# A four-layer mixed decoder trunk on one core: six edits to the order of layer 0's small VectorE work

## The chip, the cores and the metric

The kernel runs on 1 core of one Trainium2 chip. The metric is the device time of an execution in microseconds, lower is better. The engines are named TensorE (PE in rows), VectorE (DVE), ScalarE (ACT), GpSimd (POOL) and SyncE (SP), which only issues transfers here.

## The reference

A trunk of four layers over a sequence of 256 tokens of width 1024, float32. Each layer normalizes, mixes tokens, multiplies by a SiLU gate, projects out, and adds the normalized result to the stream. Layer 0 is native sparse attention, layers B, C and D are differential, dilated and stick-breaking attention. Layer 0, which the change is about:

```python
q, kc, vc, ks, vs, kw, vw, gl, z = split_cols(u @ w_in, A_SPLITS)   # 16 heads, 4 KV heads
kcmp = compress(kc, pos_k, w1_k, w2_k); vcmp = compress(vc, pos_v, w1_v, w2_v)   # 15 blocks
p_c = masked_softmax(einsum(qb, kcmp) - slopes * dist, dist >= 0); o_c = einsum(p_c, vcmp)
p_s = masked_softmax(einsum(qb, ksel) - slopes * dist, dist >= 0); o_s = einsum(p_s, vsel)
p_w = masked_softmax(einsum(qb, kwin) - slopes * dist, mask);      o_w = einsum(p_w, vwin)
o = sum(sigmoid(gl) * stack([o_c, o_s, o_w]))                       # over the three branches
return (o * silu(z)) @ w_out
```

At 256 tokens all four selection blocks of 64 are among the 16 that may be selected, and the window of 512 covers the sequence, so the selected and the window branch are both plain causal attention.

## The kernel before

**Weights.** They stream from memory by transfers that SyncE issues into the buffers `raw` (five of them; a buffer is free again when its piece's low part has been computed). Each piece of 128 x 1024 is split in two for float32 accuracy: ScalarE writes the rounded high part `whi` (L133), VectorE the low part `wlo` = raw - whi (L72). The activations are split likewise (`uth`, `utl`), and a projection is a triple of matmuls per step, L226, L227 and L228, where only L228 reads `wlo`. A projection of 256 columns (`push_proj`) has 16 steps over two pieces, and at a piece's step 0 the low parts that are due are issued.

**Layer 0.** Its attention runs in eight units p = 0 to 7 (`nsa_unit`), two heads each, with one KV group g = p // 2 for two units. `cmp_front(g)` makes the scores against the compressed keys (L789, reduced by VectorE at L793), whose softmax is a list of small operations `CHALF`: a first half L799 to L804, ended by ScalarE's exponential L805, and a second half L807 to L811. A unit's front has three slots: `first` (scores L846 and L847 of query block 0, both heads), `second` (block 1, head 0) and `finish` (block 1, head 1). Each score bank is followed by VectorE's masked maximum (L325, tile mxa) and ScalarE's exponential with its sum (L327, tile la). `scale` makes ten operations: the reciprocal and the gate product of the sums (L865) and eight scalings of P (L871). They are put in the list `SCALE` and run inside the next unit's `first`. Its back transposes P (L332), lets ScalarE evict the transposes (L172, tile PT), and weights the values (L348, L351, L888). Two score banks and two transpose banks rotate.

**Between them.** The steps of q and z projections lie in the queue `fq` and fill TensorE: `fill()` pops some after each slot, and `need(g)` pops until the projection that a unit needs lies at least six steps back. q's high part is ScalarE's L685, its low part VectorE's L686, `later` by five steps. The silu of z ends in L434; `Gate.go` multiplies the result by it (L385), and `Gate.split` cuts the product into the high and low part of the output projection's operand (L394). The output projection begins at L291.

**What sets the order.** TensorE keeps the source's order everywhere. In layer 0 (`st["own"]`), VectorE keeps it too, so the place where the source issues a small operation is its place in VectorE's queue; `later(n, f)` issues f after n more popped steps. ScalarE's, GpSimd's and SyncE's order is set by a scheduler from priorities, and outside layer 0 VectorE's as well. `low_parts(n)` issues n of the low parts that are due. In layer B, POOL's L565 finishes a mask for layer C from VectorE's L563 and L564, and L1012 and L181 make the norm for L1017 and L1024.

Of the kernel before, what the change touches and what calls it, by code (L numbers as in the profile page):

```python
# [37 lines left out]
def trunk(ctx, tc, I, out):  # L38
    nc = tc.nc
    PE, ACT, DVE, POOL = nc.tensor, nc.scalar, nc.vector, nc.gpsimd  # L40
# [37 lines left out]
    def low_parts(n):  # L78

        for i in sorted(low)[:n]:  # L80
            low.pop(i)()

    def later(n, f):

        if st["own"]:
            waiting.append((plan["count"] + n, f))
        else:
            f()
# [51 lines left out]
    def take(n):  # L140
        st["next"] += n
        return list(range(st["next"] - n, st["next"]))

    def free(*idx):
        for i in idx:
            parts.pop(i)
            st["parts" if seq[i][1] else "held"] -= 1
# [77 lines left out]
    def mm3(o, sh, sl, mh, ml, first, last):  # L225
        PE.matmul(o, sh, mh, start=first, stop=False)  # L226
        PE.matmul(o, sh, ml, start=False, stop=False)  # L227
        PE.matmul(o, sl, mh, start=False, stop=last)  # L228

    fq = deque()  # L230
    plan = {"slots": 1, "keep": 0, "count": 0}
    ready = {}
# [8 lines left out]
    def pop():  # L241
        fq.popleft()()
        plan["count"] += 1
        overdue()
# [5 lines left out]

    def need(i):

        while fq and (i not in ready or plan["count"] < ready[i] + 6):
            pop()

    def push_proj(use, q=fq, idx=None):

        t = {}
        idx = idx or take(2)

        def step(c, k):
            if c == 0 and k == 0:
                t["o"] = ps.tile([128, 2, 256], F32, name="mm", bufs=NMM)
            for i, at in ((idx[c], 0), (idx[c] + 1, 0)):
                if k == at and i in low:
                    low.pop(i)()
            wh, wl = parts[idx[c]]
            mm3(t["o"][:, c, :], wh[:, k, :], wl[:, k, :], uT[0][:, k, :], uT[1][:, k, :], k == 0, k == 7)
            if k == 7:
                free(idx[c])  # L270
                if c == 1:
                    use(t["o"])
                advance()

        for c in range(2):
            for k in range(8):
                q.append(lambda c=c, k=k: step(c, k))
# [76 lines left out]
    class Gate:  # L354
# [18 lines left out]

        def have_o(self, p):
            self.o.add(p)
            self.go()

        def go(self):
            while self.ready < 4:
# [188 lines left out]
    idx = take(8)  # L568
# [108 lines left out]
    def keep_q(o, g):  # L677


        for j in range(2):  # L680
            r, other = HALF[j], HALF[1 - j]
            hs = slice(4 * g + j, 4 * g + j + 3, 2)
            hi, sc = t["q"][r, hs, :], cq[r, 2 * g:2 * g + 1]
            with tc.high_priority(offset=EARLY):
                ACT.activation(hi, o[r], AF.Copy, scale=sc)  # L685
            later(5, lambda r=r, other=other, hs=hs, hi=hi, sc=sc: DVE.scalar_tensor_tensor(  # L686
                t["q"][other, hs, :], o[r], sc, hi.bitcast(F32), op0=OP.mult, op1=OP.subtract))
        ready[g] = plan["count"]

# [78 lines left out]
    for g in range(1, 4):  # L768
        push_proj(lambda o, g=g: keep_q(o, g))
        ga.push(g - 1)  # L770
# [9 lines left out]
    CS, PTC, CHALF, SCALE = {}, {}, [], []  # L780
# [32 lines left out]
    def mixed(*lists):  # L813

        lists = [deque(x) for x in lists]
        while any(lists):
            for x in lists:
                if x:
                    x.popleft()()
# [8 lines left out]
    def nsa_unit(p):  # L828
        g, i = divmod(p, 2)
        t = {}  # L830

        def start():
            need(g)
            t["P"] = {(j, br): work.tile([128, 384], F32, name="P", bufs=8) for j in range(2) for br in range(2)}
            t["l"], t["mx"] = small(8, "la", 3), small(8, "mxa", 3)

        def scores_of(b, js):
            if b == 0:
                start()
            n = 128 * (b + 1)  # L840
            S = {}
            for j in js:
                s = ps.tile([128, 512], F32, name="S", bufs=NSB)
                s = s[:, 0:2 * n].rearrange("p (a n) -> p a n", a=2)
                q = qT[:, 2 * p + j, b * 128:(b + 1) * 128]
                PE.matmul(s, q, KH[:, g, :, 0:n], start=True, stop=False)  # L846
                PE.matmul(s, q, KL[g // 2][:, g % 2, :, 0:n], start=False, stop=True)  # L847
                S[j] = s
            for j in js:
                for br in range(2):  # L850
                    x = (j * 2 + br) * 2 + b
                    softmax(S[j][:, br, :], causal[i], SLA[4 * g + j], 128 * b, 128 * b + n, t["P"][j, br],
                            t["mx"][:, x:x + 1], t["l"][:, x:x + 1])
# [37 lines left out]

        def first():
            scores_of(0, (0, 1))
            mixed(*(x.pop(0) for x in (SCALE, CHALF) if x))

        def second():
            scores_of(1, (0,))
            if CHALF:
                mixed(CHALF.pop(0))
            low_parts(1)  # L900

        front = [first, second, finish]
        back = [lambda: trans(0), lambda: trans(1), pvs]
# [349 lines left out]
```

## Time and profile before

| | |
|---|---|
| median of 3 runs | 579.51 us (578.88 to 580.09) |
| the profiled execution | 579.91 us, span 578.2 us, mean TensorE clock 0.995 of full speed |
| TensorE busy | 559.3 us (97%) |
| VectorE busy | 418.6 us (72%) |
| ScalarE busy | 335.0 us (58%) |
| GpSimd busy | 41.9 us (7%) |
| chain that ended last | TensorE 80%, VectorE 9%, issue 5%, ScalarE 2% |
| low parts L72 | 153, mean 1.206 us |

A busy share is an average over four layers; the stretches of layer 0's attention, from about 66 to 162 us, have to be read alone. The granted clock has two levels, 1.2 and 2.4 GHz, and the profile gives a stretch's mean as a share of the higher.

### The profile page before, as it was taken

Reading aid. Unit: us, or ns where it says so; the run is one execution under the profiler, and the core shown is the slowest. Engines: PE = TensorE matmul, PEld = TensorE weight load, DVE = VectorE, ACT = ScalarE, POOL = GpSimd, SP = SyncE. Lnnn points to the kernel's source line nnn. Section 1 sums busy time; section 2 is a strip of 40 time slices with the busy share of each in tenths; the row PEclk is TensorE's granted clock in tenths of the full one; section 3 lists DMA queues with packets and bytes.
Section 4 is the critical chain, followed back from the end, with each engine's and each line's share of the span. In section 5 each row is a group of like instructions: output and inputs, shape, how many; then the busy total and the mean of one; then the engine's idle time right before and its main releaser. Section 6 shows DMA issues by size and latency. Waiting matters only on the chain.

```text
span 578.2 us, 10454 instructions
## 1 busy us (share of the span) xinstructions
PE 559.3 (97%) x3930; PEld 495.3 (86%) x3930; DVE 418.6 (72%) x927; ACT 335.0 (58%) x719; POOL 41.9 (7%) x89
## 2 busy tenths in 40 slices
PE   7999989999999999999999999999999999999995
PEld 6997878777788799999988789999987898899984
DVE  5883696898857886777965887758548878788632
ACT  6742678788825466567643474757524855666410
POOL 1900000000101100000410100000001000000000
PEclk9999989999999999999999999999999999999999
DMA  9774632322444596443451577443525784332012
GB/s 294 259 246 152 249 110 75 129 91 86 144 154 147 177 332 210 147 147 110 146 158 62 183 270 275 150 143 117 176 73 183 257 289 140 120 108 73 2 37 73
DMA packets 27779, 90.96 MB, mean 157 GB/s; under 512 B 4560, under 2 KB 5200, under 8 KB 27728
## 3 DMA queue, kind: packets, MB, share of 16 engines
q1 hardware_dynamic: 26144, 86.09, 44.2%
q10 hardware_dynamic: 1584, 4.20, 2.3%
q8 instruction: 31, 0.51, 0.4%
q14 instruction: 20, 0.16, 0.1%
HBM read 89.22 MB, written 1.05 MB: 156 GB/s over the span
## 4 chain that ended last, share of the span: by engine, by line
PE 80%; DVE 9%; issue 5%; ACT 2%; POOL 1%; DMA 1%; SPq 0%; POOLq 0%; DVEq 0%; ACTq 0%
PE mm L226 15%; PE mm L227 14%; PE mm L228 14%; PE mm L293 7%; PE mm L292 7%; PE mm L291 7%; DVE wlo L72 4%; PE S L342 3%; PE pt L332 3%; PE o L348 2%; PE o L697 1%; DVE P L325 1%; PE pt L214 1%; DMA h<-in_x_dram 1%; ACT whi L133 1%
## 5 line engine op out<-in xcount | busy, mean ns | idle before, releaser
L226 PE MATMUL mm<-uth,whi 128*128 128x256 f32 x736 | 217.9, 296 | 0.0
L72 DVE TENSOR_TENSOR wlo<-raw,whi 128x1024 fp32r<-128x1024 f32 (+1 forms) x153 | 182.0, 1206 | 41.6 <-ACT whi L133 41.1
L227 PE MATMUL mm<-utl,whi 128*128 128x256 f32 x736 | 208.1, 283 | 0.0
L228 PE MATMUL mm<-uth,wlo 128*128 128x256 f32 x736 | 208.1, 283 | 0.0
L133 ACT ACTIVATE whi<-raw 128x1024 fp32r<-128x1024 f32 (+1 forms) x153 | 156.9, 1044 | 65.9 <-PE mm L227 33.2
L226 PEld LDWEIGHTS mm<-uth,whi 128*128 128x128 f32 x736 | 140.8, 191 | 14.2 <-issue 13.3
L227 PEld LDWEIGHTS mm<-utl,whi 128*128 128x128 f32 x736 | 141.0, 192 | 0.9
L228 PEld LDWEIGHTS mm<-uth,wlo 128*128 128x128 f32 x736 | 140.7, 191 | 0.0
L291 PE MATMUL mm<-whi,qT 128*128 128x512 f32 x128 | 50.4, 394 | 0.0
L292 PE MATMUL mm<-whi,kT 128*128 128x512 f32 x128 | 49.9, 390 | 0.0
L293 PE MATMUL mm<-wlo,qT 128*128 128x512 f32 x128 | 49.9, 390 | 0.0
L291 PE MATMUL mm<-whi,uth 128*128 128x512 f32 (+1 forms) x112 | 42.5, 380 | 0.0
L293 PE MATMUL mm<-wlo,uth 128*128 128x512 f32 (+1 forms) x112 | 42.1, 376 | 0.0
L292 PE MATMUL mm<-whi,utl 128*128 128x512 f32 (+1 forms) x112 | 42.0, 375 | 0.0
L327 ACT ACTIVATE P<-P,mxa 128x128 f32<-128x128 f32 (+1 forms) x64 | 28.4, 446 | 10.6 <-DVE mxa L325 10.5
L325 DVE CUSTOM_DVE_ANT_0 P<-S,mask 128x128 f32<-128x128 f32 (+1 forms) x96 | 29.1, 352 | 7.4 <-PE S L847 5.1
L456 ACT ACTIVATE junk<-mm 128x512 bf16<-128x512 f32 x16 | 9.5, 595 | 42.7 <-PE mm L293 42.7
L332 PE MATMUL pt<-ident,P 128*128 128x128 f32 x180 | 28.3, 280 | 1.7 <-ACT PT L172 0.8
L172 ACT ACTIVATE PT<-pt 128x384 f32<-128x384 f32 x58 | 26.1, 482 | 4.1 <-PE pt L332 3.7
L293 PEld LDWEIGHTS mm<-wlo,qT 128*128 128x128 f32 x128 | 24.0, 188 | 5.0
L291 PEld LDWEIGHTS mm<-whi,qT 128*128 128x128 f32 x128 | 24.1, 188 | 4.7
L292 PEld LDWEIGHTS mm<-whi,kT 128*128 128x128 f32 x128 | 24.1, 188 | 4.7
(206 smaller groups left out, 748.5 us busy)
## 6 DMA issues: line engine op xcount, KB each, us to landing
raw<-in_a_t_dram SPq DMA_DIRECT2D x24, 512.0 KB, 4.4
raw<-in_b_t_dram SPq DMA_DIRECT2D x24, 512.0 KB, 5.0
raw<-in_d_t_dram SPq DMA_DIRECT2D x24, 512.0 KB, 4.6
raw<-in_c_t_dram SPq DMA_DIRECT2D x20, 512.0 KB, 5.6
raw<-in_w_dram SPq DMA_DIRECT2D x8, 512.0 KB, 4.8
raw<-in_a_o_dram SPq DMA_DIRECT2D x8, 512.0 KB, 3.4
raw<-in_b_v_dram SPq DMA_DIRECT2D x8, 512.0 KB, 5.9
raw<-in_b_o_dram SPq DMA_DIRECT2D x8, 512.0 KB, 3.5
```

Of the source, the lines that this page charges most:

```text
L72: lo_of = (POOL if on_pool else DVE).tensor_tensor(lo, t, hi.bitcast(F32), op=OP.subtract)
L133: ACT.activation(hi, t, AF.Copy)
L172: ACT.activation(dst, src, AF.Copy)
L226: PE.matmul(o, sh, mh, start=first, stop=False)
L227: PE.matmul(o, sh, ml, start=False, stop=False)
L228: PE.matmul(o, sl, mh, start=False, stop=last)
L291: PE.matmul(o, sh, wh[:, j, c0:c1], start=k == 0, stop=False)
L292: PE.matmul(o, sl, wh[:, j, c0:c1], start=False, stop=False)
L293: PE.matmul(o, sh, wl[:, j, c0:c1], start=False, stop=k == 7)
L325: DVE.tensor_tensor_reduce(out=P[:, c0:c1], in0=S, in1=mask[:, c0:c1], scale=-slope, scalar=BIG, op0=OP.add, op1=OP.min, accum_out=mx)
L327: ACT.activation(P[:, c0:c1], P[:, c0:c1], AF.Exp, bias=mx, scale=-1.0, accum_out=l)
L332: PE.transpose(pt[:, i, :], P[:, i * 128:(i + 1) * 128], ident)
```

## The change

Six numbers or places in the source:

1. `need` asks for nine steps between a projection and its use, not six. It stands in every layer.
2. In `push_proj` the low part of the next piece is issued at step 3 of the current one, not at step 0.
3. `Gate.have_o` issues the gate product three steps later, not at once.
4. q's low part comes eight steps later, not five.
5. `first` runs the first six operations of `SCALE` (two for the sums, four scalings of branch 0) alone, and mixes only the other four with `CHALF`'s first half. Before, all ten were mixed.
6. `second` issues no low part where there is a `CHALF` half to run, and two where there is none. Before, it issued one in either case.

```diff
     def need(i):
 
-        while fq and (i not in ready or plan["count"] < ready[i] + 6):
+        while fq and (i not in ready or plan["count"] < ready[i] + 9):
             pop()
...
-            for i, at in ((idx[c], 0), (idx[c] + 1, 0)):
+            for i, at in ((idx[c], 0), (idx[c] + 1, 3)):
                 if k == at and i in low:
                     low.pop(i)()
...
         def have_o(self, p):
             self.o.add(p)
-            self.go()
+            later(3, self.go)
...
-            later(5, lambda r=r, other=other, hs=hs, hi=hi, sc=sc: DVE.scalar_tensor_tensor(
+            later(8, lambda r=r, other=other, hs=hs, hi=hi, sc=sc: DVE.scalar_tensor_tensor(
...
             scores_of(0, (0, 1))
-            mixed(*(x.pop(0) for x in (SCALE, CHALF) if x))
+            ops = SCALE.pop() if SCALE else []
+            mixed(ops[:6])
+            mixed(ops[6:], CHALF.pop(0) if CHALF else [])
...
             if CHALF:
                 mixed(CHALF.pop(0))
-            low_parts(1)
+            else:
+                low_parts(2)
```

On VectorE, at the start of the units: L724 and L727 prepare the compressed branch's second layer, L739 and L747 end it, L793 is the first reduction of unit 0's compressed scores, L325 its first masked maximum. This is one piece of the difference.

```order
 L686 SCALAR_TENSOR_TENSOR qT<-mm,cq,qT 64x2x256 x2
-L72 TENSOR_TENSOR wlo<-raw,whi 128x1024
 L724 COPY P<-pt 128x120
 L727 COPY zw<-pt 128x240 x2
+L72 TENSOR_TENSOR wlo<-raw,whi 128x1024
 L739 SCALAR_TENSOR_TENSOR kc<-S,kc 128x4x15
 L747 TENSOR_TENSOR v<-o,bm 60x256 x4
 L793 TENSOR_REDUCE cs<-S 128x120
-L72 TENSOR_TENSOR wlo<-raw,whi 128x1024
 L325 ISA P,mxa<-S,mask 128x128
```

One low part moved behind the copies, and the one ahead of the first maximum left.

On ScalarE, in the same place (L685 is q's high part, L327 the exponentials of unit 0, L805 that of its compressed scores):

```order
 L685 ACTIVATE qT<-mm,cq 64x2x256 x2
-L133 ACTIVATE whi<-raw 128x1024
-L327 ACTIVATE P,la<-P,mxa 128x128 x4
+L327 ACTIVATE P,la<-P,mxa 128x128 x4
+L133 ACTIVATE whi<-raw 128x1024
 L805 ACTIVATE cs<-cs 128x120
-L327 ACTIVATE P,la<-P,mxa 128x256 x2
-L133 ACTIVATE whi<-raw 128x1024
-L327 ACTIVATE P,la<-P,mxa 128x256 x2
+L327 ACTIVATE P,la<-P,mxa 128x256 x4
```

The high part L133 moved from ahead of the four exponentials to between them and L805. In unit 2 it is alike: the rows from L685 to L327 there, before and after.

```order
L685 ACTIVATE qT<-mm,cq 64x2x256 x2
L172 ACTIVATE PT<-pt 128x384 x2
L805 ACTIVATE cs<-cs 128x120
L133 ACTIVATE whi<-raw 128x1024
L172 ACTIVATE PT<-pt 128x384 x2
```

```order
L685 ACTIVATE qT<-mm,cq 64x2x256 x2
L172 ACTIVATE PT<-pt 128x384 x2
L133 ACTIVATE whi<-raw 128x1024
L172 ACTIVATE PT<-pt 128x384 x2
L805 ACTIVATE cs<-cs 128x120
```

L805 moved behind the high part and the second pair of evictions.

On VectorE, at the end of the units, where L940 to L944 (three more in the changed source) make layer B's lambda from a small load: the rows of before, then of after.

```order
L72 TENSOR_TENSOR wlo<-raw,whi 128x1024
L940 ISA P,lam<-P 128x64
L940 ISA lam 128x1
L865 RECIPROCAL la<-la 128x8
L865 TENSOR_TENSOR la<-la,gate 128x8
L871 TENSOR_SCALAR P<-P,la 128x128
...
L434 SCALAR_TENSOR_TENSOR zw<-zw,mm 128x512
L943 TENSOR_TENSOR lam<-lam 128x1
L385 SCALAR_TENSOR_TENSOR oT<-oT,zw 128x512
L394 TENSOR_TENSOR kT<-oT,qT 128x512 x3
```

```order
L72 TENSOR_TENSOR wlo<-raw,whi 128x1024
L434 SCALAR_TENSOR_TENSOR zw<-zw,mm 128x512
L943 ISA P,lam<-P 128x64
L943 ISA lam 128x1
L385 SCALAR_TENSOR_TENSOR oT<-oT,zw 128x512
L865 RECIPROCAL la<-la 128x8
...
L865 TENSOR_TENSOR la<-la,gate 128x8
L871 TENSOR_SCALAR P<-P,la 128x128
...
L394 TENSOR_TENSOR kT<-oT,qT 128x512 x3
```

The last silu and a gate product moved from behind unit 7's scaling to ahead of it.

## Rows read from the trace of the kernel before

**Rows 1.** Busy times by stretch: start:end us, length, each engine's busy us, TensorE's clock, DMA.

```profile
70.00:80.00 10.00, 7.62 (x57) 7.02 (x56) 9.65 (x36) 6.37 (x18) 0.00 (x0) 1.00 0.28 96
...
120.00:130.00 10.00, 8.96 (x71) 7.32 (x71) 9.79 (x39) 7.98 (x25) 0.00 (x0) 1.00 0.36 107
```

**Rows 2.** TensorE's waits, whole run: tile and line, releaser: us in total, times, longest.

```profile
PE S L846 <- DVE mxa L325: 4.3, 5, 2.1
...
PE pt L1024 <- DVE ob L1017: 1.1, 1, 1.1
```

**Rows 3.** TensorE's timeline, units 0 to 5: start, us, line op, idle before, releaser.

```profile
67.86 0.66 PE L735 MATMUL S<-P,w 128*128 128x60 f32 x4 [0.53 <-DVE P L724]
...
76.57 0.28 PE L226 MATMUL mm<-uth,whi 128*128 128x256 f32 x1
...
76.93 0.28 PE L226 MATMUL mm<-uth,whi 128*128 128x256 f32 x1
...
80.18 0.36 PE L846 MATMUL S<-kT,qT 128*128 128x256 f32 x1 [2.13 <-DVE mxa L325]
...
105.66 0.47 PE L846 MATMUL S<-kT,qT 128*128 128x512 f32 x1 [0.80 <-DVE mxa L325]
...
125.76 0.47 PE L846 MATMUL S<-kT,qT 128*128 128x512 f32 x1 [0.62 <-DVE mxa L325]
...
128.83 0.92 PE L332 MATMUL pt<-ident,P 128*128 128x128 f32 x6 [0.42 <-ACT PT L172]
```

**Rows 4.** Busy times by stretch, around the lower clock.

```profile
81.40:84.80 3.40, 3.10 (x14) 2.84 (x14) 3.33 (x19) 2.21 (x8) 0.00 (x0) 0.53 0.48 159
```

**Rows 5.** VectorE's timeline, units 0 and 1.

```profile
71.31 1.21 DVE L72 TENSOR_TENSOR wlo<-raw,whi 128x1024 fp32r<-128x1024 f32 x1
72.44 0.28 DVE L325 CUSTOM_DVE_ANT_0 P<-S,mask 128x128 f32<-128x128 f32 x1
...
77.71 1.51 DVE L686 SCALAR_TENSOR_TENSOR qT<-mm,cq,qT 64x512 fp32r<-64x512 f32 x2
```

**Rows 6.** ScalarE's timeline, units 0 to 3.

```profile
72.44 1.06 ACT L133 ACTIVATE whi<-raw 128x1024 fp32r<-128x1024 f32 x1
...
74.94 0.29 ACT L805 ACTIVATE cs<-cs 128x120 f32<-128x120 f32 x1
...
97.39 0.88 ACT L172 ACTIVATE PT<-pt 128x384 f32<-128x384 f32 x2
98.29 0.30 ACT L805 ACTIVATE cs<-cs 128x120 f32<-128x120 f32 x1
98.50 1.04 ACT L133 ACTIVATE whi<-raw 128x1024 fp32r<-128x1024 f32 x1
```

**Rows 7.** VectorE's timeline, before unit 3's maxima.

```profile
103.27 1.22 DVE L72 TENSOR_TENSOR wlo<-raw,whi 128x1024 fp32r<-128x1024 f32 x1
104.41 0.68 DVE L385 SCALAR_TENSOR_TENSOR oT<-oT,zw 128x512 f32<-128x512 f32 x1
```

**Rows 8.** Timeline, last q low parts and the scores that read them.

```profile
132.56 1.53 DVE L686 SCALAR_TENSOR_TENSOR qT<-mm,cq,qT 64x512 fp32r<-64x512 f32 x2
...
134.06 1.04 PE L789 MATMUL S<-kc,qT 128*128 128x32 f32 x8
```

**Rows 9.** Timeline, VectorE at layer 0's tail, then TensorE's first output projection.

```profile
150.65 0.23 DVE L940 CUSTOM_DVE_ANT_0 P<-P 128x64 f32<-128x64 f32 x1 [1.21 <-DMA P<-in_b_lambda_dram]
...
153.30 1.93 DVE L871 TENSOR_SCALAR P<-P,la 128x128 f32<-128x128 f32 x8
...
161.56 0.40 PE L291 MATMUL mm<-whi,qT 128*128 128x512 f32 x1
```

**Rows 10.** Timeline, VectorE's mask row and GpSimd's behind it, layer B.

```profile
287.54 0.35 DVE L564 TENSOR_SCALAR P<-P 128x384 f32<-128x384 int32 x1
...
288.03 2.47 POOL L565 TENSOR_TENSOR mask<-mask,P 128x384 f32<-128x384 f32 x1 [4.15 <-DVE P L564]
```

## The prediction

> **What bounds the kernel now.** I read the busy times by stretch first. TensorE is busy almost all of the span, so a change of order can save only its idle time and the time at the lower clock. From 70 to 80 us it is busy for 7.62 of 10 us while VectorE is busy for 9.65, and from 120 to 130 for 8.96 against 9.79 [rows 1]: here, in layer 0, VectorE sets the pace. The list of TensorE's waits says the same. Its score matmuls (L846) wait 4.3 us in five places for VectorE's mxa, which is the row maximum whose reading frees the score bank, and in layer B L1024 waits 1.1 us once [rows 2]. These, with what each stall drags behind it, are about all that can be had. The timeline gives each stall its place: 0.53 at L735, then at L846 2.13 (unit 1), 0.80 (unit 3) and 0.62 (unit 5), with 0.75 left for the two others of the five, and 0.42 at a transposition L332 that waits for ScalarE [rows 2, 3]. In all 5.2 us. From 81.4 to 84.8 the granted clock is 0.53, so mostly at 1.2 GHz, after the stretch with the two longest stalls; 3.10 us of matmuls there would take about half at 2.4 GHz [rows 4].
>
> **Units 0 and 1: -0.93.** The low part L72 that stood before L735's source now comes behind it, so 0.53 goes. The next L72 leaves the front of the first softmax: its 1.13 (71.31 to 72.44, where the maxima begin) comes off VectorE's chain [rows 3, 5]. That is 1.66. Some is given back on ScalarE, which the change moves too. Before, L133 (72.44) stood ahead of the four exponentials; now it stands between them and the exponential L805 of the compressed branch, which VectorE needs for L807 [rows 6]. ScalarE cannot begin the four before L685 ends, so L805 falls only some 0.9 earlier and VectorE idles about 0.73: 1.66 - 0.73 = 0.93. One L72 and the q low parts of 77.71, 1.51 for two, stay ahead of unit 0's last maxima [rows 5], so the 2.13 stall is moved and not removed: the low part for the gate projection's second piece now comes later than its first L228, and TensorE waits there instead. Ends: 0 (all given back) and -1.66.
>
> **Units 2 and 3: -0.18.** L72 (1.14 to the next start) and the gate product L385 (0.68, of which about 0.6 to the next start), 1.74 together, leave the front of unit 3's maxima [rows 7], and the 0.80 of stall is the most that TensorE can gain [rows 3]. But ScalarE's L805, at 98.29 before, comes behind L133 and the second pair of evictions [rows 6]: 1.7 us later by the 1.04 of the L133 at 98.50 and a pair such as the one before L805 (0.88 at 97.39), less the 0.2 by which neighbours overlap. VectorE then idles for some 1.5 of its 1.74. I take -0.18 between 0 and -0.80.
>
> **Units 4 to 7: -0.40.** The stalls 0.62 and 0.42 [rows 3] shrink for the same reason, but L72 and L385 land in unit 5 ahead of the last q low parts. Those end at 134.09 (132.56 + 1.53) and L789, which reads them, starts at 134.06: there is no slack now [rows 8]. The margin of nine puts three more projection steps ahead of L789 (0.36 each by two neighbours, 76.57 and 76.93 [rows 3], 1.07 for three), about what the 1.74 less the gain asks for. Ends 0 and -1.04.
>
> **Tail of layer 0: +0.75.** Counted on VectorE from unit 7's last but one maxima to its last scaled P: before, L72, the wait of 1.21 for the lambda load at L940, maxima, L72, the sums and the scaling [rows 9]; after, a second L72 (1.14) fills that wait and L434 with L385 (two products of L385's shape, about 0.6 each [rows 7]) stands ahead of the scaling. Added 2.34, taken off 1.21: +1.14. The last transpositions come that much later against the rest, and three projection steps (1.07) that covered such lateness have been spent. TensorE's own work carries part of it before L291 at 161.56; I take 0.75 at L291, between 0 and 1.14 + 1.07 = 2.2.
>
> **The scaling in two pieces: 0.** Eight scalings take 1.93 [rows 9] whether or not small operations are mixed in. What mixing hides is the chain of five small operations; taken out for four scalings it costs VectorE about 0.3 (an estimate: five at some 0.06), three times. Those four are what the first transposition reads and come earlier; the last P comes as before. Ends -0.3 and +0.9.
>
> **Layer B: -0.60.** The margin holds in every layer. In layer B the masks' arithmetic (L563, L564) is moved ahead of the last unit's scaling, while before it came at 287.54 and let GpSimd begin its 2.47 us only at 288.03, ahead of the norm that L1017 and L1024 wait for [rows 10]. Without it the 1.1 [rows 2] goes; one step of cover less costs 0.36, and the scaling itself is a little later. 1.08 - 0.36 = 0.72, taken as 0.60, between -1.08 and +0.36. **The other layers**: no waits at scores, so three steps earlier change nothing there; +0.1, between 0 and +0.3.
>
> Sum: -0.93 - 0.18 - 0.40 + 0.75 - 0.60 + 0.10 = -1.26. The profiled execution took 579.91 (578.2 of span and 1.7 around it), 0.40 above the median 579.51. So 578.65 on its footing and 578.25, say **578.3**, on the median's.
>
> **Rivals.** *The clock stays up.* If units 0 and 1 run with less idle time, the stretch at 0.53 is gone: half of 3.10 us, of which VectorE, busy 3.33 of 3.40 there, hides a little [rows 4], leaving 1.2: 578.25 - 1.2 = 577.0. For it: a stall of 0.62 at 125.76 and TensorE at 8.96 of 10 did not lower the clock (1.00 there) [rows 1, 3]. Against: a stall of 2 us remains by my count. The Trainium skill, TensorE: Matmul & The Clock Gate, What's actually happening, says that a gate passes half or all of the pulses by how busy the array has been; that agrees with the two levels in rows 4, and it makes this case hang on whether the moved stall joins the one behind it. By that page the drop stays if they join. *The gains are given back.* If ScalarE's new order holds L805 longer than I took, the first three terms go to about 0.2 together: -1.26 + 1.3 = 0, 579.5. For it: VectorE at 9.65 of 10 has the same work to do, only in another order. *Slower, by the tail.* The gate product ahead of the last scaling delays the whole chain of transposition, weighting, product and split that ends in L291. If VectorE and not TensorE has the last word there, the full 2.2 counts in place of 0.75: +1.45; if besides the q low parts make L789 wait, units 4 to 7 lose their 0.40: -1.26 + 1.45 + 0.40 = +0.6, and with the unit 0 gain halved +1.1: 580.6. It decides as soon as VectorE reaches unit 7's scaling no more than 1.1 us earlier than now. *The change does not do what it says:* excluded by the order, in which the rows have moved.
>
> **How the numbers follow.** 0.2% is 1.16 us, about what a measurement of this kernel can tell from no change: faster is below 578.35, slower above 580.67. The forecast has 0.42, own range 577.4 to 579.2, so half of it falls under the bound; the clock 0.25 at 577.0, all faster; given back 0.15 at 579.5; slower 0.18 at 580.6, reaching to 581.6 where the scaling's +0.9 is added, some of it within the bound. Faster 0.21 + 0.25 = 0.46, rounded up for the lower end of the third case to 0.47; slower 0.14; within 0.39. The range 576.3 to 580.7 takes in the clock case with a layer B at its best end (577.0 - 0.5, rounded) and the nearer half of the slow one.
>
> **What would show it.** In the profile after: no wait at L735; a wait at the first L228 of the gate projection near 74 to 77 us; L846's wait of 2.13 shorter or gone; VectorE idle before L807 twice, released by ScalarE's L805; no wait at L1024, with GpSimd's L565 done by 288; and L291 some 0.8 us before 161.56. The granted clock between 78 and 86 tells the first two cases apart. I am wrong if L291 falls later than 161.56, or if layers C and D move by over 0.3.

## The result: 1.65% slower, and the profile after

| | before | after |
|---|---|---|
| median of 4 runs | 579.8 us (578.88 to 580.29) | 589.6 us (587.53 to 590.01) |
| ratio | | 1.0165, 95% interval 1.0145 to 1.0185 |
| the profiled execution, its span | 579.91, 578.2 | 589.25, 587.5 |
| mean granted clock of the span | 0.995 | 0.986 |

The forecast was 578.3, and the range to 580.7 did not hold the time. TensorE's waits of the whole run after (tile and line, releaser: us in total, times, longest):

```profile
PE mm L228 <- DVE wlo L72: 2.5, 1, 2.5
PE S L846 <- DVE mxa L325: 1.9, 3, 0.8
PE o L1006 <- ACT PT L172: 1.8, 1, 1.8
PE pt L332 <- DVE P L871: 1.8, 2, 1.5
...
PE pt L332 <- ACT PT L172: 1.6, 3, 1.1
```

The waits at L735 and at L1024 [rows 2, 3] are gone, and the one at L846 has fallen from 4.3 to 1.9. In their place stand one of 2.54 at L228, the transpositions L332, and 1.8 at the weighting of layer B (L1006, before L1003). The waits behind the first layer's norm that differ between the two lists make 11.1 us after and 6.7 before: 4.4 of the 9.3 us of span. The rest does not show as waits. The ten us in which [rows 4] lie and three later stretches (start:end, length, busy us of TensorE, its weight loads, VectorE, ScalarE and GpSimd, then TensorE's clock):

```profile
80.00:90.00 10.00, 9.63 (x80) 8.30 (x79) 9.01 (x31) 8.96 (x27) 0.00 (x0) 1.00 0.42 136
150.00:160.00 10.00, 7.39 (x43) 4.98 (x45) 6.80 (x24) 6.20 (x14) 1.57 (x4) 0.74 0.41 150
160.00:170.00 10.00, 10.00 (x48) 8.49 (x47) 1.93 (x3) 2.56 (x4) 0.00 (x0) 0.75 0.00 0
290.00:300.00 10.00, 7.72 (x49) 7.36 (x50) 7.53 (x16) 3.17 (x8) 1.21 (x2) 0.83 0.33 105
```

The clock is at 1.00 from 80 to 90, where before it was down [rows 4], and falls at the end of layer 0's units instead: 0.74 and 0.75 in two stretches of 10 us, so about half of both at 1.2 GHz. It falls once more in layer B. This is layer 0's tail on TensorE (start, length, line, operation, idle time before and its releaser):

```profile
153.32 1.07 PE L332 MATMUL pt<-ident,P 128*128 128x128 f32 x6 [1.49 <-DVE P L871]
155.50 1.54 PE L332 MATMUL pt<-ident,P 128*128 128x128 f32 x6 [1.12 <-ACT PT L172]
156.97 1.12 PE L348 MATMUL o<-PT,v 128*64 128x256 f32 x4
...
165.62 0.40 PE L291 MATMUL mm<-whi,qT 128*128 128x512 f32 x1
```

Unit 6 ends at 150.6. Three projection steps are left ahead of unit 7's transpositions. Then the first transposition waits 1.49 for VectorE's scaling, the second, right behind it, 1.12 for the eviction that frees a transpose bank, and the weighting follows with no step between. Before, four steps stood ahead of the first transposition, one between the two and one behind them, and there was no wait:

```profile
153.74 1.07 PE L332 MATMUL pt<-ident,P 128*128 128x128 f32 x6
...
156.56 0.65 PE L348 MATMUL o<-PT,v 128*64 128x256 f32 x4
```

From 156.97 on the same four matmuls of L348 take 1.12 us (0.65 before), and L291 starts at 165.62, where it stood at 161.56 [rows 9]. From that L348 to L291 the work is the same in both, and it takes 8.65 us after and 5.00 before: 3.65 us that show as no wait. Up to the tail the change gains: the compressed scores of the second to the last group start at 90.17, 112.22 and 132.56.

```profile
77.13 0.38 PE L228 MATMUL mm<-uth,wlo 128*128 128x256 f32 x1 [2.54 <-DVE wlo L72]
...
90.17 0.96 PE L789 MATMUL S<-kc,qT 128*128 128x32 f32 x8
...
112.22 0.96 PE L789 MATMUL S<-kc,qT 128*128 128x32 f32 x8
...
132.56 0.18 PE L789 MATMUL S<-kc,qT 128*128 128x32 f32 x1
```

In before's trace those three starts were at 92.07, 114.32 and 134.06 (the last in [rows 8]), so the lead is 1.9, 2.1 and 1.5 (the last with 1.07 us of steps done earlier besides). All of that and 4.1 us more are lost between 132 and 166 us. By the starts of the output projections (L291) in the two traces, layer B then loses 3.0 us and layer D 2.3, and layer C nothing. The start of a trace is itself good for a us or two: in five of the thirteen traces of this case the clock falls between 12 and 20 us, ahead of anything that the edits touch, and L291's first start lies between 17.6 and 20.1 us. For these two it is 18.0 and 18.2.

### The profile page after: what moved, and what is told of

It is laid out like the page before. It is cut to its first block, busy times and chain, and to the rows that moved or that the text cites. A ratio compares the mean times of both kernels' runs of the same rounds, so it can differ in the third digit from the quotient of the medians.

```text
span 587.5 us, 10450 instructions
## 1 busy us (share of the span) xinstructions
PE 564.2 (96%) x3930; PEld 499.7 (85%) x3930; DVE 418.5 (71%) x927; ACT 335.2 (57%) x719; POOL 39.4 (7%) x89
## 4 chain that ended last, share of the span: by engine, by line
PE 73%; DVE 12%; issue 6%; ACT 3%; DMA 2%; POOL 2%; SPq 0%; POOLq 0%; DVEq 0%; ACTq 0%
PE mm L226 14%; PE mm L227 13%; PE mm L228 13%; PE mm L291 6%; PE mm L292 6%; PE mm L293 6%; DVE wlo L72 4%; PE S L342 3%; PE pt L332 3%; PE o L348 2%; DVE P L325 2%; DVE P L871 1%; ACT whi L133 1%; PE o L697 1%; DMA h<-in_x_dram 1%
## 5 line engine op out<-in xcount | busy, mean ns | idle before, releaser
L228 PE MATMUL mm<-uth,wlo 128*128 128x256 f32 x736 | 209.1, 284 | 2.5 <-DVE wlo L72 2.5
L72 DVE TENSOR_TENSOR wlo<-raw,whi 128x1024 fp32r<-128x1024 f32 (+1 forms) x153 | 181.6, 1205 | 35.7 <-ACT whi L133 35.0
L133 ACT ACTIVATE whi<-raw 128x1024 fp32r<-128x1024 f32 (+1 forms) x153 | 157.0, 1044 | 77.4 <-PE mm L227 41.5
L228 PEld LDWEIGHTS mm<-uth,wlo 128*128 128x128 f32 x736 | 141.8, 193 | 2.7 <-DVE wlo L72 2.7
L291 PE MATMUL mm<-whi,qT 128*128 128x512 f32 x128 | 50.4, 394 | 0.0
L291 PE MATMUL mm<-whi,uth 128*128 128x512 f32 (+1 forms) x112 | 42.6, 380 | 0.0
L327 ACT ACTIVATE P<-P,mxa 128x128 f32<-128x128 f32 (+1 forms) x64 | 28.5, 447 | 11.0 <-DVE mxa L325 10.8
L325 DVE CUSTOM_DVE_ANT_0 P<-S,mask 128x128 f32<-128x128 f32 (+1 forms) x96 | 29.1, 352 | 7.1 <-PE S L342 5.4
L332 PE MATMUL pt<-ident,P 128*128 128x128 f32 x180 | 28.2, 284 | 4.2 <-DVE P L871 1.8
L291 PEld LDWEIGHTS mm<-whi,qT 128*128 128x128 f32 x128 | 24.1, 188 | 4.7
L172 ACT ACTIVATE PT<-pt 128x384 f32<-128x384 f32 x58 | 25.6, 480 | 3.2 <-PE pt L332 2.9
```

The source lines that it names most:

```text
L72: lo_of = (POOL if on_pool else DVE).tensor_tensor(lo, t, hi.bitcast(F32), op=OP.subtract)
L133: ACT.activation(hi, t, AF.Copy)
L172: ACT.activation(dst, src, AF.Copy)
L291: PE.matmul(o, sh, wh[:, j, c0:c1], start=k == 0, stop=False)
L325: DVE.tensor_tensor_reduce(out=P[:, c0:c1], in0=S, in1=mask[:, c0:c1], scale=-slope, scalar=BIG, op0=OP.add, op1=OP.min, accum_out=mx)
L327: ACT.activation(P[:, c0:c1], P[:, c0:c1], AF.Exp, bias=mx, scale=-1.0, accum_out=l)
```

## The experiments

Each kernel was timed against the kernel before on the same chip at about the same time; its medians lie between 579.4 and 579.9, so kernels timed at different times compare to about half a us. The kernels with "margin" in their names have q's low part with it where the text says so: it comes eight steps after the high part in the changed kernel, and with a margin of six the scores would be issued ahead of it.

### The margin, and the rest without it

```diff
-        while fq and (i not in ready or plan["count"] < ready[i] + 9):
+        while fq and (i not in ready or plan["count"] < ready[i] + 6):
...
-            later(8, lambda r=r, other=other, hs=hs, hi=hi, sc=sc: DVE.scalar_tensor_tensor(
+            later(5, lambda r=r, other=other, hs=hs, hi=hi, sc=sc: DVE.scalar_tensor_tensor(
```

> The changed kernel with the margin back at six steps and q's low part back at five (the two go together: with six and eight the compressed scores would read q before its low part is issued). The other four edits stay. Theory M, the margin: all of the loss comes from the three projection steps that are spent early, in the tails of layers 0, B and D; the other edits only gain. Then units 0 to 5 are 2.4 to 3 us ahead of the kernel before, layer 0's tail has its steps between the transpositions again and does not lose them, and the time is 576.5 to 578. Theory V, VectorE's new order: the low parts and the gate product at other steps delay the tail; then the time stays at 585 to 589.

Measured: 580.34 against 579.55, ratio 1.0016 (1.0000 to 1.0032). 9 of the 10 us are gone, so the margin, with q's later low part, is in nearly all of the loss. But 577 was not reached. The profiled execution, the fastest of ten at 578.62, has TensorE some 3 us ahead at unit 5, 0.3 of it from an earlier start, and L291 keeps 1.3 (160.22 against 161.56): L789 waits 1.3 for q's low part near 131, and behind that the clock falls (0.83 from 130 to 140), where in before's trace it fell behind 80. The ten runs lie between 578.62 and 582.29, with mean clocks from 0.994 down to 0.986, where the kernel before has 0.992 to 0.998. So what the four edits save in waits goes in part with a lower clock; the clock does not order these ten runs by itself (582.29 was at 0.992).

The kernel before with the margin alone:

```diff
-        while fq and (i not in ready or plan["count"] < ready[i] + 6):
+        while fq and (i not in ready or plan["count"] < ready[i] + 9):
```

> The kernel before with the margin of nine and nothing else. Theory M: the losses of the changed kernel without its gains, 590 to 593, with TensorE's waits at layer 0's last transpositions, at layer B's last unit and the slower weighting in layer D. Theory V: 579 to 581, since VectorE's order of low parts is that of before.

Measured: 586.39 against 579.55, 1.0109 (1.0088 to 1.0131). One number of the six costs 6.8 us. Theory V, by which VectorE's new order is the cause, is out for the greater part; theory M's 590 was too high, since its reckoning left no part of the changed kernel's loss to the two together. 6.8 from the margin alone and 0.8 from the rest alone make 7.6; 9.8 was measured. About 2 us come only with both, near the limit of what the intervals tell apart. The traces show where: with the margin alone, unit 7's transpositions wait 0.48 and 0.56, not 1.49 and 1.12, the clock stays at 1.00 from 150 to 170, and from L348 (157.37) to L291 (162.42) it is 5.05.

```profile
154.88 1.07 PE L332 MATMUL pt<-ident,P 128*128 128x128 f32 x6 [0.48 <-DVE P L871]
156.51 0.93 PE L332 MATMUL pt<-ident,P 128*128 128x128 f32 x6 [0.56 <-ACT PT L172]
```

The other edits bring TensorE to the tail 2.6 us earlier (unit 6's L888 at 149.92, there at 152.49) and VectorE's last scaling only 1.6 (L871 at 152.88, there at 154.45). So part of what they gain turns into wait, and behind the wait the clock falls.

The margin of nine in layer 0 alone, in the changed kernel:

```diff
-        while fq and (i not in ready or plan["count"] < ready[i] + 9):
+        while fq and (i not in ready or plan["count"] < ready[i] + (9 if st["own"] else 6)):
```

> The changed kernel with the margin of nine in layer 0 alone and six in layers B, C and D. Theory M in all its places: layer 0 keeps its +3.5 us, the some 3 us of layer B's tail, 1 of its head and 2.2 of layer D go, 582 to 584. If the lower clock and the late tail of layer 0 are what delays the later layers, nothing is gained: 587 to 590.

Measured: 582.51 against 579.55, 1.0050 (1.0029 to 1.0071). As theory M expected, the later layers hold most of the loss. By the traces 5.3 us are there: layers B and D take as long as in the kernel before. The rest of the 7.1 lies in the tail of layer 0, which is the same in both kernels: here the clock fell for a shorter time, and from L348 to L291 it is 6.5 us and not 8.65. Why it fell for less is not shown; the ten runs of this kernel go from 579.46 to 585.13.

### Layers B and D by themselves

In both, the kernel before gets the margin of nine in one layer:

```diff
-        while fq and (i not in ready or plan["count"] < ready[i] + 6):
+        while fq and (i not in ready or plan["count"] < ready[i] + st.get("margin", 6)):
...
+    st["margin"] = 9
+
     def stick_unit(p):
```

> The kernel before with the margin of nine in layer D alone. If the margin's price there is its own (ScalarE makes a high part ahead of the transposes' evictions, so that the second head's weighting starts after the first's, 0.32 us in each of some seven units), the time is 2.2 us above the kernel before, 581.5 to 582.3. If layer D's loss is carried over from what happened earlier, it stays within 0.5 of before.

Measured: 581.74 against 579.39, 1.0030 (1.0017 to 1.0043): 2.35 us, in a layer where TensorE never shows a wait at its scores. The rows put the cause on ScalarE. Layer D of the changed kernel, first ScalarE, then TensorE:

```profile
509.60 1.04 ACT L133 ACTIVATE whi<-raw 128x1024 fp32r<-128x1024 f32 x1
510.55 0.85 ACT L172 ACTIVATE PT<-pt 128x384 f32<-128x384 f32 x2
...
508.96 0.82 PE L332 MATMUL pt<-ident,P 128*128 128x128 f32 x6
...
511.13 0.76 PE L348 MATMUL o<-PT,v 128*64 128x256 f32 x3
...
511.94 0.38 PE L351 MATMUL o<-PT,v 128*64 128x128 f32 x2
```

The transpositions end at 509.5, but ScalarE does a high part (L133) first and evicts both transposes from 510.55 to 511.40. The two heads of a unit use the two halves of the array's columns and run side by side. Before, ScalarE was done with its high part when the transpositions ended at 501.37, the evictions stood next, and both heads began together:

```profile
499.67 1.04 ACT L133 ACTIVATE whi<-raw 128x1024 fp32r<-128x1024 f32 x1
...
501.07 0.87 ACT L172 ACTIVATE PT<-pt 128x384 f32<-128x384 f32 x2
...
502.72 0.65 PE L348 MATMUL o<-PT,v 128*64 128x256 f32 x4
503.20 0.39 PE L351 MATMUL o<-PT,v 128*64 128x128 f32 x4
```

Four L348 and four L351 ran from 502.72 to 503.59 there, 0.87 us. Now the second head begins 0.32 later than the first, as its eviction ends, and the eight run for 1.19. In five of the eight units it is these 0.32, in a sixth 0.38 with a wait of 0.2: 2.0 of the 2.3 us. Otherwise no wait row shows it, because TensorE's first matmul finds its operand ready: the loss is in the pairing. TensorE's own order has not changed there: in both kernels 24 projection matmuls stand between these units' scores and their transpositions, and 12 between these and the weighting. What the margin moves is the phase: the high parts fall at another place of each unit, and since such a unit takes 16 steps, as many as a projection has, it is the same place in the next. A run with the high part put behind the evictions was not made.

The same edit with the line ahead of `diff_unit`, and the margin back at six ahead of layer C:

> The kernel before with the margin of nine in layer B alone. If the price in layer B is the margin's own (the last unit's scaled P comes late for lack of cover, then its eviction stands on ScalarE behind a high part of the gate product that waits for VectorE, and the clock falls), the time is 2.5 to 3.5 us above before, 582 to 583, with waits at L332 and at the weighting L1003. If it is brought about by layer 0's tail, within 0.5 of before.

Measured: 580.96 against 579.50, 1.0022 (1.0005 to 1.0039). 1.5 us, less than I expected; in its trace the clock stays at 1.00 in layer B, where the changed kernel shows 0.83 from 290 to 300. From L291 of layer 0 to L291 of layer B it is 135.0 us in the kernel before, 136.5 here and 138.0 in the changed kernel. So half of layer B's 3.0 us are its waits and half the lower clock behind them, which comes in some traces and not in others. The waits are the same:

```profile
284.95 0.74 PE L332 MATMUL pt<-ident,P 128*128 128x128 f32 x3 [0.80 <-DVE P L995]
...
288.96 0.49 PE L1005 MATMUL o<-v,PT 128*128 128x128 f32 x2 [1.84 <-ACT PT L172]
...
287.90 0.63 ACT L393 ACTIVATE qT<-oT 128x512 fp32r<-128x512 f32 x1 [3.49 <-DVE oT L385]
288.44 0.47 ACT L172 ACTIVATE PT<-pt 128x384 f32<-128x384 f32 x1
```

Two queues make them. VectorE's mask arithmetic (L563, L564) stands ahead of the last unit's scaling, as the prediction said, but it waits there for GpSimd's iota, so the scaled P comes late. And ScalarE has the split of a gate product (L393) ahead of the eviction (L172): it sits 3.49 us until VectorE has made the product, with the finished transposes behind it. Before, the eviction stood ahead of the split:

```profile
286.13 0.47 ACT L172 ACTIVATE PT<-pt 128x384 f32<-128x384 f32 x1
...
287.65 0.63 ACT L393 ACTIVATE qT<-oT 128x512 fp32r<-128x512 f32 x1 [1.04 <-DVE oT L385]
```

The changed kernel shows the rows of the margin's kernel 5.5 us later in its trace, VectorE's wait for GpSimd first:

```profile
286.84 1.16 DVE L563 TENSOR_SCALAR P<-P 128x384 int32<-128x384 int32 x1 [0.78 <-POOL P L562]
...
293.39 0.63 ACT L393 ACTIVATE qT<-oT 128x512 fp32r<-128x512 f32 x1 [3.49 <-DVE oT L385]
...
294.45 0.54 PE L1006 MATMUL o<-v,PT 128*128 128x128 f32 x2 [1.84 <-ACT PT L172]
```

### The tail of layer 0: clock, order or cover

Idle matmuls in the waits of the changed kernel's tail:

```diff
         def trans(br):
+            if p == 7:
+                s = ps.tile([128, 512], F32, name="S", bufs=NSB)
+                for _ in range((12, 8)[br]):
+                    PE.matmul(s[:, 0:128], ident, ident, start=True, stop=True)
```

> The changed kernel with idle matmuls of the identity on a score bank that nobody reads: 12 ahead of unit 7's first transpositions and 8 between these and the second, where TensorE waited 1.49 and 1.12 us. They take about 0.11 us each at the full clock, 1.3 and 0.9 us, so they fit into the waits. Theory K, the clock: most of layer 0's loss in the tail is the 10.2 us at half clock that follow the waits; with TensorE busy the clock stays up, L291 comes 3 to 5 us earlier and the time is 584.5 to 587. Theory C, the cover: the lost time is the waits themselves; the clock is a symptom, and the time stays at 588.5 to 590.5.

Measured: 585.87 against 579.87, 1.0103 (1.0089 to 1.0116), some 3.7 us less than the changed kernel's 589.6 (timed separately, against a before of 579.8). The added work was more than I had reckoned, since each of these matmuls is two on TensorE, 2.84 and 1.95 us:

```profile
152.49 2.84 PE L878 MATMUL S<-ident 128*128 128x128 f32 x24
155.17 0.82 PE L332 MATMUL pt<-ident,P 128*128 128x128 f32 x6
155.83 1.95 PE L878 MATMUL S<-ident 128*128 128x128 f32 x16
...
158.36 0.65 PE L348 MATMUL o<-PT,v 128*64 128x256 f32 x4
...
163.48 0.40 PE L291 MATMUL mm<-whi,qT 128*128 128x512 f32 x1
```

One of its stretches, read as those of the changed kernel above:

```profile
156.00:160.00 4.00, 4.00 (x40) 3.52 (x41) 1.63 (x5) 1.96 (x5) 0.00 (x0) 1.00 0.02 6
```

L332 begins 1.9 us later than in the changed kernel and L291 still 2.1 earlier; 0.9 of the lateness is from the start of the execution. From L348 to L291 it is 5.12 us, not 8.65. The clock stayed at 1.00 with nothing changed but that TensorE was busy, the four runs have mean clocks of 0.993 to 0.996 where the changed kernel's have 0.983 to 0.990, and the time fell: the lower clock, 3.65 us, is the larger part of the tail's loss of 6.6 (worked out below), and it follows from the idle time. Theory K holds, theory C does not. Not all of the 3.7 us are the tail's, though: in this trace layer 0 is 3.0 us shorter than in the changed kernel's, and layer B 1.5, because there too the clock stayed at 1.00; the later start takes 0.9 of it back. Whether filling the tail is what spared layer B is not shown.

The scaling back ahead of the silu and the gate product:

```diff
             SCALE.append(scale())
+            if p == 7:
+                mixed(SCALE.pop())
...
-        units = [nsa_unit(p) for p in range(8)] + [([lambda: mixed(SCALE.pop()), *[lambda: None] * 2], None)]
+        units = [nsa_unit(p) for p in range(8)] + [([lambda: mixed(SCALE.pop() if SCALE else []), *[lambda: None] * 2], None)]
```

> The changed kernel with unit 7's scaling run on VectorE right behind its last low part, ahead of the silu and the gate product, as it stood before the change. Margin and TensorE's order stay. If the product ahead of the scaling is a cause of its own, TensorE's wait of 1.49 at the transposition is gone, the time falls by 1.2 for it and by up to 4 where the lower clock goes with it: 584 to 588. If the missing steps alone count (they are still missing), the wait moves to the evictions behind and the time stays at 588.5 to 590.

Measured: 584.71 against 579.87, 1.0081 (1.0067 to 1.0094), 4.9 us under the changed kernel. So the order in the tail counts too: L291 comes at 161.53, the clock is at 1.00 there, and the wait for the eviction is 0.78:

```profile
153.42 1.07 PE L332 MATMUL pt<-ident,P 128*128 128x128 f32 x6 [1.06 <-DVE P L873]
...
156.00 0.55 PE L332 MATMUL pt<-ident,P 128*128 128x128 f32 x3 [0.78 <-ACT PT L172]
...
161.53 0.40 PE L291 MATMUL mm<-whi,qT 128*128 128x512 f32 x1
```

The first wait is still 1.06; it was not taken away as I had expected. The scaled P's come no sooner in this trace than in the changed kernel's (the last scaling starts at 152.99, against 152.88 there), for its units ran some 0.5 us later. What comes sooner is ScalarE's first eviction. In the changed kernel a high part stands ahead of both evictions; here one eviction comes before that high part (154.51), and the second transposition begins at 154.67 and not at 155.50. The changed kernel's two rows, then this one's:

```profile
154.01 1.06 ACT L133 ACTIVATE whi<-raw 128x1024 fp32r<-128x1024 f32 x1 [0.47 <-PE pt L332]
154.97 0.85 ACT L172 ACTIVATE PT<-pt 128x384 f32<-128x384 f32 x2
...
154.13 0.49 ACT L172 ACTIVATE PT<-pt 128x384 f32<-128x384 f32 x1 [0.57 <-PE pt L332]
```

So in the tail of layer 0, as in layers B and D, work of ScalarE ahead of an eviction holds TensorE up. In either repair, busy TensorE or the earlier eviction, the clock stayed up in the tail and, in the profiled executions, in layer B; layer B then loses 1.5 us and layer D 2.3, together 3.8.

That the gate product stands there is the margin's doing, and not that of edit 3:

```diff
         def have_o(self, p):
             self.o.add(p)
-            later(3, self.go)
+            self.go()
```

> The changed kernel with the gate product issued at once, as before. Theory M: within 0.5 us of the changed kernel, 588 to 590, since the product stands ahead of the last scaling for the margin's sake and not for this edit's. Theory V: some 1.3 us of VectorE go from the tail's chain and the lower clock with it, 583 to 586.

Measured: 588.59 (585.21 to 589.74) against 579.55, 1.0143 (1.0111 to 1.0175). By the medians theory M's value; the fastest of the four runs, at a clock of 0.995, is 585.21, so by itself this run leaves room for a gain of a microsecond or two by edit 3's removal. In the tail, VectorE's silu and gate product stand ahead of the scaling in this kernel as in the changed one, and in the kernel with the margin alone too.

### The moved wait in unit 0, and a better kernel

The changed edits with the margin of six, and one number between:

```diff
-            for i, at in ((idx[c], 0), (idx[c] + 1, 3)):
+            for i, at in ((idx[c], 0), (idx[c] + 1, 1)):
```

> The changed kernel with the margin and q's low part of before, and the next piece's low part at step 1 of the current one, not at step 3 (nor 0). VectorE then makes it between the two halves of unit 0's compressed softmax and not behind both. Theory K: the changed edits without the margin save 2 us of waits but put 2.5 of them in one piece at the gate projection's first L228, after which the clock falls in more executions; with the piece's low part 2 us earlier that wait falls to about 0.5 to 1, the mean granted clock is back at 0.995 or more, and the time is 576.5 to 578.5. If the wait is only moved to the next score matmul, 579 to 580.5.

Measured: 579.31 against 579.87, 0.9995 (0.9980 to 1.0010). The wait at L228 is gone, and TensorE waits at L846 instead, 1.8 us: it was moved, as the second expectation had it. The twelve runs fall in groups by mean clock: 577.76 to 579.31 at 0.994, 579.12 to 579.57 at 0.991, 581.01 to 581.62 at 0.989. The trace, of the execution of 581.01 us, has a stretch at 1.2 GHz behind each of three places: one at 12 to 20 us, ahead of anything edited, the wait at 80 us, and one at the compressed scores of the last group. That last one is q's low part, which has L72, L72, the gate product and L72 ahead of it on VectorE:

```profile
133.85 0.28 PE L789 MATMUL S<-kc,qT 128*128 128x32 f32 x1 [0.80 <-DVE qT L686]
134.63 0.95 PE L789 MATMUL S<-kc,qT 128*128 128x32 f32 x7 [0.50 <-DVE qT L686]
```

The one-number change in the kernel before:

```diff
-            for i, at in ((idx[c], 0), (idx[c] + 1, 0)):
+            for i, at in ((idx[c], 0), (idx[c] + 1, 1)):
```

> The kernel before with one number changed: the next piece's low part at step 1, not 0. It takes the low parts from ahead of L735's source and of the first maxima and puts one behind the compressed softmax's first half. The 0.53 at L735 and the 0.43 at L846 go, the wait of 2.13 stays or shrinks by up to 1: 578 to 579.3. If VectorE's total before unit 1 is what counts, within 0.3 of before.

Measured: 579.83 against 579.39, 1.0006 (0.9995 to 1.0017). No gain: L846's waits add to 4.3 us there as before, in three pieces instead of five, and the longest is 2.9 where it was 2.13. It is the outcome that the second expectation ties to VectorE's total, 0.4 us above before and not 0.3.

The kernel before the last one (step 1, with edits 3, 5 and 6), with the mixed scaling of before, and the last q low part two steps after its high part:

```diff
-            ops = SCALE.pop() if SCALE else []
-            mixed(ops[:6])
-            mixed(ops[6:], CHALF.pop(0) if CHALF else [])
+            mixed(*(x.pop(0) for x in (SCALE, CHALF) if x))
...
-            later(5, lambda r=r, other=other, hs=hs, hi=hi, sc=sc: DVE.scalar_tensor_tensor(
+            later(2 if g == 3 else 5, lambda r=r, other=other, hs=hs, hi=hi, sc=sc: DVE.scalar_tensor_tensor(
```

> The last kernel with the next piece's low part at step 1, with the scaling mixed as before the change and the last KV group's q low part two steps after its high part, not five, so that it stands ahead of a low part of the weights. The waits of 0.8 and 0.5 at the compressed scores L789 near 134 us shrink to under 0.5, the stretch at half clock behind them goes, and the time is 577 to 578.5. If VectorE only hands the same delay to unit 5's last maxima, L846 waits in their place and it is 579 to 580.

Measured: 578.24 against 579.39, 0.9978 (0.9967 to 0.9989), 0.2% faster than the kernel before, with an interval that leaves out one. No wait is left at L789, no stretch at half clock behind it, and L846's waits for the maxima are 2.1 in two places, with 0.5 more for L793's reading:

```profile
PE S L846 <- DVE mxa L325: 2.1, 2, 1.7
```

It keeps edits 3 and 6 of the change, a third of edit 2, and neither the margin nor the unmixed scaling. It gains 1.15 us over the kernel before as timed beside it; the kernel with the unmixed scaling and q's low part at five steps gained 0.56 over its own. Which of the two steps brought the difference was not told apart, and the two intervals overlap.

## Why the prediction was wrong, point by point

**What bounds the kernel** was right: VectorE sets the pace in the units, and TensorE's waits in layer 0 were 5.6 us (the prediction's 5.2 leaves out a second 0.42 at L332) and the one in layer B 1.1. The lower end of the range is 576.5 by its own working, not 576.3.

**Units 0 and 1** were right in every event, and too high in size. L735's wait went, VectorE idled before L807 for L805's sake (0.67, forecast 0.73), and L228 waited 2.54 near 77 us. The lead at L789 of group 1 was 1.9 and not 0.93, but most of it is luck with the clock: the stretch at half clock [rows 4] did not come in this execution. Nor did it come in the execution of the kernel with the margin of nine in layer B alone, whose layer 0 is that of before (its two L789):

```profile
69.54 1.06 PE L789 MATMUL S<-kc,qT 128*128 128x32 f32 x8
...
90.82 0.96 PE L789 MATMUL S<-kc,qT 128*128 128x32 f32 x8
```

That is 21.28 us from the first group's scores to the second's with the clock at 1.00, where before's trace has 22.59 (69.48 to 92.07) and the changed kernel's 21.25 (68.92 to 90.17). So the stretch at half clock costs 1.3 us, near the 1.2 of the rival *the clock stays up*, and the change of order gains the 0.53 at L735 and next to nothing more. In the changed layer 0, too, the stretch came in some traces (margin nine in layer 0 alone: 0.7 us less lead; gate product at once: 2.0 less).

```profile
74.70 0.28 DVE L807 TENSOR_REDUCE cl<-cs 128x8 f32<-128x120 f32 x1 [0.67 <-ACT cs L805]
...
98.43 0.28 DVE L807 TENSOR_REDUCE cl<-cs 128x8 f32<-128x120 f32 x1 [1.35 <-ACT cs L805]
```

**Units 2 to 5**: for units 2 and 3, -0.18 forecast, -0.20 measured from L789 to L789 (a lead of 1.90, then 2.10); VectorE's idle time before L807 was 1.35 there, forecast 1.5 (the second row). For units 4 to 7 -0.40, and units 4 and 5 brought 0.47 (to 1.50 and the 1.07 of steps done ahead). L789 of the last group waited 0.47, where none was put down.

**The tail of layer 0** is the step that failed first: +0.75, between 0 and 2.2, against +6.6 (from a lead of 2.57, the steps counted, to a lag of 4.06 at 165.62). VectorE's part of it was right: counted on from where unit 7's maxima stood (146.32, 1.22 ahead of 147.54) the last scaled P was due at 155.15 - 1.22 + 1.14 = 155.07, and VectorE's next instruction started at 154.72. Wrong was the sentence that the missing steps cost their own 1.07 at most and that TensorE's own work carries part of the lateness. With the steps went what lay between the two transpositions, so that the second waits for ScalarE to free a bank (1.12), and between them and the weighting. TensorE, ahead by more than a microsecond, had the wait of the whole chain to itself: busy for 1.57 of 4 us from 152 to 156. That cost the clock for some 10 us, and 3.65 us of time between L348 and L291; the waits and the transpositions make up the rest. Both the idle matmuls and the scaling put first show it: with either the clock stays up and that stretch is 5.1 us. The size is this execution's: with the same layer 0 the stretch took 6.5 us in the trace of the margin in layer 0 alone. I had the clock as a rival at the other end of the layer, where it could only help, and never asked it of the place that the change laid bare.

```profile
152.00:156.00 4.00, 1.57 (x9) 1.18 (x10) 3.96 (x16) 3.35 (x6) 0.00 (x0) 0.85 0.61 229
156.00:160.00 4.00, 4.00 (x23) 2.56 (x23) 0.83 (x4) 0.98 (x2) 0.00 (x0) 0.50 0.00 0
```

**Layer B**: -0.60 against +3.0, of which 1.5 are waits and 1.5 the clock. The mechanism was seen and its sign missed. The mask arithmetic did move ahead of the scaling, L1024's wait did go; but I let the move cost nothing ("a little later"), where it waits for GpSimd and holds the scaled P, and did not look at what stands before the eviction on ScalarE.

**The other layers**: +0.1 against +2.3, all in layer D. "No waits at scores" was true and beside the point: the margin moves the pieces of the projections against the units, and so the high part on ScalarE to a place ahead of the two evictions.

**The scaling in two pieces**: 0, not tested by itself. On VectorE it was sized well: in unit 2 the way from the sums' reciprocal to the next maxima took 3.25 us (93.06 to 96.31), where it took 2.86 (94.96 to 97.82), against the estimate of 0.3 more.

**The clock.** The Trainium skill, TensorE: Matmul & The Clock Gate, What's actually happening, says that the gate is set by how busy the array has been recently. The traces agree: in all thirteen the stretches at half clock follow stretches in which TensorE was less busy, and filling one kept the clock at 1.00. What no row of before could show is how readily the clock falls: after the wait of 2.54 near 77 us it fell in three traces and not in three others, of kernels that are alike there.

**The rivals.** "Slower, by the tail" named the place and the chain and was given 0.18; its price stopped at +1.1, for want of the clock. The condition set for it, that VectorE reaches unit 7's scaling no more than 1.1 us earlier than now, was met: L871 starts at 152.88, 0.42 before the 153.30 of [rows 9]. Both signs of being wrong came: L291 fell later than 161.56, and layer D moved by 2.3.

## What to carry to other kernels

A margin that fetches filler work forward takes it from somewhere: find the places it leaves, and there count the chain of every engine, evictions and banks included, with no filler at all. In three layers here ScalarE's queue had its part: what stands ahead of an eviction there holds TensorE up. A lead that ends in a bare tail is turned into idle time, and idle time can turn into a lower clock that costs more than the wait did (3.65 us behind waits of 2.6). An edit to a number that all layers read has to be priced in each of them, also where the profile shows no wait.

## What the runs showed of the hardware that was not expected

- The mean granted clock differs between executions of one kernel, and the time with it: the kernel with the margin of nine in layer 0 ran 580.31 us at 0.999 and 585.13 at 0.987. The kernel before ran 578.24 at 0.998 and 580.43 at 0.992, though the slowest execution beside these, 581.07, was at 0.996. The same layer 0 took 1.3 us less from L789 to L789 where the clock stayed at 1.00, and the same waits in layer B were followed by a lower clock in some traces and not in others (138.0 and 136.5 us). A shift of 1 us can thus be a matter of the clock alone, and a kernel that waits less in sum can lose by waiting longer in one place.
- The two column halves of the array ran a pair of weightings in 0.87 us when both operands were there and in 1.19 when the second came 0.32 later: no wait was shown, and TensorE counted as busy 10 of 10 us from 500 to 510.
